# Sums of weight quarters in a decoder layer's token mixing, made on VectorE instead of by accumulating DMAs

## The chip, the cores and the metric

The kernel runs on one core of a Trainium2 chip. The metric is the device time of one execution in microseconds. Three runs of the kernel before gave 1376.22, 1376.38 and 1378.35 us; the median is 1376.38 us. One further execution was recorded by the hardware profiler: 1376.86 us, of which the span from the first to the last instruction is 1375.1 us. Everything below that has a place in time ("at 611.13 us") is counted from the start of that span.

## The reference

One decoder layer: a half-step feed-forward, token mixing in three gated branches, a second half-step feed-forward, with a normalisation before and behind each. There are 512 tokens, a model width of 1024 and a feed-forward width of 2816, all in float32.

```python
def swiglu(x, w_gu, w_down):
    g, u = jnp.split(x @ w_gu, 2, axis=-1)
    return (jax.nn.silu(g) * u) @ w_down

def token_mixing(u, mem, w_in, ...):
    proj = u @ w_in
    hq, hf, hi, hog, dcols, mq, gl = jnp.split(proj, SPLITS, axis=-1)
    o_hg = rmsnorm(hgrn2(hq, hf, hi, lb), hg_norm_w)
    ...
    y_dil = dilated_attention(dcols)
    y_mem = memory_attention(mq, mem, mem_norm_w, w_mem_kv)
    ...
    y = (gates[:, :, 0] * (y_hg @ w_br_hg)
         + gates[:, :, 1] * (y_dil @ w_br_dil)
         + gates[:, :, 2] * (y_mem @ w_br_mem))
    return y @ w_out

def reference(...):
    h = h + 0.5 * rmsnorm(swiglu(rmsnorm(h, ffn1_pre_w), ffn1_w_gu, ffn1_w_down), ffn1_post_w)
    u = rmsnorm(h, mix_pre_w)
    y = token_mixing(u, mem, w_in, ...)
    h = h + rmsnorm(y, mix_post_w)
    h = h + 0.5 * rmsnorm(swiglu(rmsnorm(h, ffn2_pre_w), ffn2_w_gu, ffn2_w_down), ffn2_post_w)
```

What matters here are the wide projections `x @ w_gu` and `u @ w_in`.

## The kernel before

**Seven products for a pair of columns.** Most of both projections is done for two blocks of 128 weight columns at a time (`pair`). The 1024 x 256 piece of the weights is seen as 2 x 2 quarters of 512 x 128: `a11` and `a12` are the two halves of the first column block, `a21` and `a22` those of the second. The tokens are split in two halves of 256 as well, and seven products of quarters take the place of eight. Four of the seven need a sum of quarters as their weight: `s1 = a21 + a22`, `s3 = a21 + a11`, `s2 = s1 + a11`, `s4 = s2 + a12`. Products 1, 2 and 4 take `a11`, `a12` and `a22` as they are; 5, 6, 3 and 7 take s1, s2, s4 and s3. Product j is asked for in the order 1, 6, 5, 7, 2, 3, 4.

**Splitting.** For precision each weight quarter is split into a high part (ScalarE, line 161) and the rest (VectorE, line 162 by way of `tt`, line 158), and each product is 12 matmuls of 256 columns (lines 353 to 355): high by high, high by low, low by high, for four pieces of 128 rows. A pair is thus 84 such matmuls, 7 splits, and some additions of its results (`pair` and `pair_out`, lines 358 to 392), from which other work goes on.

**Loading.** `wops` (line 285) loads a pair: `st` (a11 and a12, 512 KB, 4 buffers, shared with other weights) and `sh` (a22, 256 KB, 2 buffers) come through SyncE's DMA queue. The quarter a21 is loaded twice, into two buffers of the five named `sum`, and GpSimd then issues an accumulating DMA onto each (line 302), which adds a22 to the one and a11 to the other; these are s1 and s3. s2 and s4 are made by VectorE when they are asked for (line 309). `pairs` (line 321) calls `wops` one pair ahead of the pair that is being computed.

**What calls it.** `ffn` uses pairs for the feed-forward weights (20 pairs in each of two), `hgrn_pair`, `dil_pair`, the step of the memory queries and `branch` for the columns of `w_in` (32 pairs in all). In `dil_pair` (line 912) six pairs follow each other; each makes the queries and keys of one attention head, and the scores (line 340, four small matmuls a head, tile `px`) follow a few microseconds behind each pair. Behind the last pair of a group the author calls for the outstanding scores at once, before anything else:

```python
            for i, (hd, nb, s0, s12, st0, st1) in enumerate(heads):
                self.need(*scores[i])
                t_dil.append(self.spawn(self.dil_values(hd, s0, s12, st0, st1, v, y_dil)))
```

`branch` has a pair and then 24 matmuls of 512 columns for two outputs.

**What sets the order.** The author writes the order of tasks; side tasks (scores, softmax, HGRN2 steps) are generators that are woken after so many microseconds of matmuls have been issued (`tick`, the table LAT). From that program a scheduler lays out one list of instructions per engine. On the chip each engine and each DMA queue works strictly through its own list: an instruction that waits holds up all that stand behind it on the same engine. GpSimd's list holds the accumulating DMAs, the small DMAs that exchange softmax statistics between heads' layouts (tiles `x` and `ot`, lines 756 to 761), the powers of the normalisation (line 181) and some memsets.

**Names in the trace.** `sum<-sh` is the accumulating DMA that makes s1, `sum<-st` on POOL the one that makes s3, `sum<-sum,st` on DVE an addition for s2 or s4. `w<-st,w`, `w<-sum,w` and `w<-sh,w` are the low parts of splits; `w<-sh,w`, the split of a22, is the last use of an `sh` buffer and frees it. `s<-s,s`, `s<-s,ps` and `s<-ps,s` of 256 columns are additions of a pair's results. `ps<-xhi,w` and the like are the matmuls of a pair, `px<-s,s` (line 340) among others those of the scores.

## Time and profile before

| | |
|---|---|
| median of 3 runs (lowest to highest) | 1376.38 us (1376.22 to 1378.35) |
| profiled execution | 1376.86 us |
| its span | 1375.1 us |
| TensorE (PE) busy | 1333.8 us, 97% |
| VectorE (DVE) busy | 1015.6 us, 74% |
| ScalarE (ACT) busy | 742.5 us, 54% |
| GpSimd (POOL) busy | 161.9 us, 12% |
| bytes moved by DMA | 210.95 MB |

The token mixing runs from about 350 to 990 us, with its first normalisation at 355 to 390 us, the two groups of `dil_pair` at about 575 to 653 us and 700 to 774 us on TensorE, the pairs of the memory queries between them, and the three calls of `branch` from 774 us. The rest is feed-forward. Busy time of TensorE overlaps from one matmul to the next, so an engine that is 97% busy can still lose a little time in gaps that the waits don't list; SyncE only issues DMAs, and has no busy time.

### The profile page before, as it was taken

How to read it: one execution, taken by the hardware profiler on the slowest of the kernel's cores; microseconds unless marked ns; L12 is line 12 of the kernel's file. 1: busy time of each engine (PE TensorE's matmuls, PEld its weight loads, DVE VectorE, ACT ScalarE, POOL GpSimd, SP SyncE). 2: the span in 40 equal slices, each digit the busy share in tenths (PEclk: the TensorE clock that was granted, in tenths of full speed). 3: DMA queues.
4: the chain of work that ended last, by engine and by line, in shares of the span. 5: the costliest groups of instructions: out<-in, count | busy, mean ns of one | idle time of the engine just before them, and what ended most of it. 6: DMA issues, size and time to landing. Idle time of an engine off the chain costs nothing.

```text
span 1375.1 us, 24568 instructions
## 1 busy us (share of the span) xinstructions
PE 1333.8 (97%) x9197; PEld 1236.2 (90%) x9197; DVE 1015.6 (74%) x1932; ACT 742.5 (54%) x1527; POOL 161.9 (12%) x204
## 2 busy tenths in 40 slices
PE   6999999999999999998999999999999999999997
PEld 6999999999788888897899999999889999999995
DVE  6877777777787875576877787787478877777765
ACT  6665544555466755354645665565366655445541
POOL 1111111110111110111201211010021111111101
PEclk9999999999999999999999999999999999999999
DMA  9676565555547535576546666665465875656513
GB/s 268 146 174 184 150 153 140 147 149 160 188 116 214 154 92 171 156 156 158 119 124 164 147 146 162 147 161 139 129 208 122 189 187 148 153 138 153 140 47 138
DMA packets 264238, 210.95 MB, mean 153 GB/s; under 512 B 10645, under 2 KB 216886, under 8 KB 264118
## 3 DMA queue, kind: packets, MB, share of 16 engines
q1 hardware_dynamic: 241142, 168.41, 41.2%
q0 software_dynamic: 21248, 37.82, 16.8%
q10 hardware_dynamic: 1728, 3.15, 0.6%
q8 instruction: 72, 1.18, 0.4%
q14 instruction: 48, 0.39, 0.1%
HBM read 162.12 MB, written 9.47 MB: 125 GB/s over the span
## 4 chain that ended last, share of the span: by engine, by line
PE 43%; DVE 4%; DMA 3%; issue 2%; ACT 1%; POOL 1%; SPq 0%; DVEq 0%; POOLq 0%; ACTq 0%
PE ps L353 8%; PE ps L355 8%; PE ps L354 8%; PE ps L334 3%; PE ps L333 3%; PE ps L335 3%; PE px L334 2%; PE px L333 2%; PE px L335 2%; PE px L340 2%; DVE s L158 1%; DVE w L158 1%; DMA sh<-in_w_in_dram 1%; PE px L344 1%; DMA sum<-sh 1%
## 5 line engine op out<-in xcount | busy, mean ns | idle before, releaser
L161 ACT ACTIVATE w<-sum 128x512 fp32r<-128x512 f32 x288 | 180.2, 631 | 221.0 <-PE ps L354 171.8
L158 DVE TENSOR_TENSOR w<-sum,w 128x512 fp32r<-128x512 f32 x288 | 196.2, 687 | 83.4 <-ACT w L161 81.7
L353 PE MATMUL ps<-xhi,w 128*128 128x256 f32 x864 | 247.1, 286 | 1.9 <-ACT s L371 1.9
L355 PE MATMUL ps<-xhi,w 128*128 128x256 f32 x864 | 245.7, 284 | 0.0
L354 PE MATMUL ps<-xlo,w 128*128 128x256 f32 x864 | 245.2, 284 | 0.0
L161 ACT ACTIVATE w<-st 128x512 fp32r<-128x512 f32 x260 | 163.3, 630 | 135.2 <-PE ps L354 97.1
L158 DVE TENSOR_TENSOR w<-st,w 128x512 fp32r<-128x512 f32 x260 | 177.0, 687 | 42.0 <-ACT w L161 40.5
L158 DVE TENSOR_TENSOR s<-s,s 128x256 f32<-128x256 f32 (+3 forms) x316 | 176.7, 564 | 17.2 <-ACT s L161 4.2
L353 PEld LDWEIGHTS ps<-xhi,w 128*128 128x128 f32 x864 | 166.2, 192 | 4.8 <-ACT s L371 2.1
L354 PEld LDWEIGHTS ps<-xlo,w 128*128 128x128 f32 x864 | 166.3, 192 | 2.4 <-issue 0.2
L355 PEld LDWEIGHTS ps<-xhi,w 128*128 128x128 f32 x864 | 166.4, 193 | 0.0
L302 POOL DMA_DIRECT2D sum<-st x72 | 62.8, 872 | 618.7 <-DVE s L158 312.4
L158 DVE TENSOR_TENSOR sum<-sum,st 128x512 f32<-128x512 f32 x144 | 99.1, 688 | 42.5 <-issue 31.8
L158 DVE TENSOR_TENSOR s<-s,ps 128x256 f32<-128x256 f32 (+1 forms) x194 | 92.1, 476 | 33.8 <-PE ps L335 25.9
L333 PE MATMUL px<-s,s 128*128 128x512 f32 x288 | 112.6, 391 | 0.0
L334 PE MATMUL px<-s,s 128*128 128x512 f32 x288 | 112.5, 391 | 0.0
L335 PE MATMUL px<-s,s 128*128 128x512 f32 x288 | 112.1, 389 | 0.0
L302 POOL DMA_DIRECT2D sum<-sh x72 | 63.2, 877 | 272.3 <-DMA sh<-in_w_in_dram 104.3
L353 PE MATMUL ps<-t3hi,w 128*128 128x256 f32 x288 | 82.6, 287 | 0.7 <-DVE s L158 0.7
L353 PE MATMUL ps<-t4hi,w 128*128 128x256 f32 x288 | 82.2, 285 | 0.0
L354 PE MATMUL ps<-t3lo,w 128*128 128x256 f32 x288 | 82.1, 285 | 0.0
L353 PE MATMUL ps<-t2hi,w 128*128 128x256 f32 x288 | 81.9, 284 | 0.0
(185 smaller groups left out, 3417.7 us busy)
## 6 DMA issues: line engine op xcount, KB each, us to landing
st<-in_ffn_w_gu_dram SPq DMA_DIRECT2D x48, 512.0 KB, 4.7
st<-in_w_in_dram SPq DMA_DIRECT2D x48, 512.0 KB, 3.9
st<-in_ffn_w_down_dram SPq DMA_DIRECT2D x44, 512.0 KB, 4.0
sum<-in_ffn_w_gu_dram SPq DMA_DIRECT2D x80, 256.0 KB, 3.4
sum<-sh POOLq DMA_DIRECT2D x72, 256.0 KB, 3.8
sum<-st POOLq DMA_DIRECT2D x72, 256.0 KB, 3.8
sum<-in_w_in_dram SPq DMA_DIRECT2D x64, 256.0 KB, 3.1
sh<-in_ffn_w_gu_dram SPq DMA_DIRECT2D x40, 256.0 KB, 3.6
```

What stands on the lines that cost most here:

```text
L158: self.pin(self.nc.vector.tensor_tensor(out=out, in0=a, in1=b, op=op))
L161: self.pin(self.nc.scalar.activation(hi, src, AF.Copy))
L302: self.nc.gpsimd.dma_start(out=u, in_=x, accum_op=ALU.add)
L333: mm(out, lhsT=lhs[0], rhs=rhs[0], start=first, stop=False)
L334: mm(out, lhsT=lhs[0], rhs=rhs[1], start=False, stop=False)
L335: mm(out, lhsT=lhs[1], rhs=rhs[0], start=False, stop=last)
L340: self.nc.tensor.matmul(out, lhsT=lhsT, rhs=rhs, start=start, stop=stop, **k)
L344: self.nc.tensor.transpose(out, in_, self.ident)
L353: mm(out, lhsT=lh, rhs=rh, start=first and k == 0, stop=False, skip_group_check=True)
L354: mm(out, lhsT=lh, rhs=rl, start=False, stop=False, skip_group_check=True)
L355: mm(out, lhsT=ll, rhs=rh, start=False, stop=k == 3, skip_group_check=True)
```

## The change

In the token mixing `wops` loads a21 once, into one `sum` buffer, and issues no accumulating DMA. When s1 is asked for, VectorE makes it as `a21 + a22` in a buffer of its own, and when s3 is asked for, VectorE adds a11 to a21 in place. The feed-forward calls `pairs` with `by_load=True` and keeps its two loads and two accumulating DMAs. For 32 pairs this takes away 32 loads of 256 KB, 64 accumulating DMAs of 256 KB and their 64 entries in GpSimd's list, and adds 64 VectorE additions of 128 x 512.

```diff
--- before.py
+++ after.py
@@ -282,7 +282,7 @@
                 out += [(hi[:, i, :], lo[:, i, :]) for i in range(per)]
         return out
 
-    def wops(self, w, c1, c2):
+    def wops(self, w, c1, c2, by_load):
 
 
 
@@ -296,15 +296,23 @@
         def new_sum():
             return self.wpool.tile([P, 4, P], F32, tag="sum", bufs=NSUM, name=f"sum{self.uid()}")
 
-        for n, x in (("s1", a22), ("s3", a11)):
-            u = new_sum()
-            self.bring(u, quarter(0))
-            self.nc.gpsimd.dma_start(out=u, in_=x, accum_op=ALU.add)
-            sums[n] = u
+        if by_load:
+            for n, x in (("s1", a22), ("s3", a11)):
+                u = new_sum()
+                self.bring(u, quarter(0))
+                self.nc.gpsimd.dma_start(out=u, in_=x, accum_op=ALU.add)
+                sums[n] = u
+        else:
+            a21 = sums["a21"] = new_sum()
+            self.bring(a21, quarter(0))
 
         def total(n):
+            if n == "s3" and n not in sums:
+                total("s1")
+                self.tt(a21, a21, a11, ALU.add)
+                sums[n] = a21
             if n not in sums:
-                a, b = {"s2": ("s1", a11), "s4": ("s2", a12)}[n]
+                a, b = {"s1": ("a21", a22), "s2": ("s1", a11), "s4": ("s2", a12)}[n]
                 u = new_sum()
                 self.tt(u, total(a), b, ALU.add)
                 sums[n] = u
@@ -318,11 +326,11 @@
             return ops[j]
         return get
 
-    def pairs(self, specs):
+    def pairs(self, specs, by_load=False):
 
         ahead = None
         for x in specs:
-            now, ahead = ahead, self.wops(*x)
+            now, ahead = ahead, self.wops(*x, by_load)
             if now:
                 yield now
         yield ahead
@@ -417,7 +425,7 @@
         y = [[self.slot() for _ in range(2)] for _ in range(NT)]
         gw = self.col_tiles(w_gu, 0, plain)
         uw = self.col_tiles(w_gu, DFF, plain)
-        pairs = self.pairs([(w_gu, f * P, DFF + f * P) for f in range(plain, NF)])
+        pairs = self.pairs([(w_gu, f * P, DFF + f * P) for f in range(plain, NF)], True)
 
         def swiglu(sg, su, act):
             nc.scalar.activation(sg, sg, AF.Silu)
```

The scheduler lays the lists out anew. Three places of it follow; the numbers behind the names tell buffers and tiles apart.

VectorE's list at the end of the first `dil_pair` group, from the split of a22 of its last pair (tile sh1549 before, sh1548 after), which frees an `sh` buffer, to the sums of the pair that is loaded into that buffer next (sh1646 in both, a pair of memory queries). Before:

```order
L158 TENSOR_TENSOR w1599_7713<-sh1549_7446,w1598_7712 128x512
L158 TENSOR_TENSOR s1546_7442<-s1554_7456,ps1562_7496 128x4x64
L158 TENSOR_TENSOR w1615_7801<-st1607_7787,w1614_7800 128x512
L158 TENSOR_TENSOR s1547_7443<-ps1565_7514,s1554_7456 128x4x64
L158 TENSOR_TENSOR w1620_7823<-sum1618_7819,w1619_7822 128x512
L158 TENSOR_TENSOR w1623_7841<-sum1609_7791,w1622_7840 128x512
L158 TENSOR_TENSOR s1579_7596<-s1578_7595,ps1582_7614 128x256
L158 TENSOR_TENSOR w1626_7859<-sum1610_7794,w1625_7858 128x512
L158 TENSOR_TENSOR sum1660_8010<-sum1647_7944,st1645_7940 128x512
```

After:

```order
L158 TENSOR_TENSOR w1599_7701<-sh1548_7432,w1598_7700 128x512
L158 TENSOR_TENSOR s1545_7428<-s1552_7438,ps1561_7480 128x4x64
L158 TENSOR_TENSOR w1614_7785<-st1607_7775,w1613_7784 128x512
L158 TENSOR_TENSOR s1546_7429<-ps1564_7498,s1552_7438 128x4x64
L158 TENSOR_TENSOR w1620_7809<-sum1617_7803,w1619_7808 128x512
L158 TENSOR_TENSOR sum1660_7994<-sum1647_7931,sh1646_7929 128x512
L158 TENSOR_TENSOR sum1647_7931<-sum1647_7931,st1645_7927 128x512
L158 TENSOR_TENSOR w1623_7827<-sum1618_7804,w1622_7826 128x512
L158 TENSOR_TENSOR s1578_7581<-s1577_7580,ps1581_7599 128x256
L158 TENSOR_TENSOR w1626_7846<-sum1609_7779,w1625_7845 128x512
L158 TENSOR_TENSOR sum1659_7993<-sum1660_7994,st1645_7927 128x512
L158 TENSOR_TENSOR sum1658_7992<-sum1659_7993,st1645_7927 128x512
```

Between the freeing split and the first sum of the later pair stood seven instructions, and now stand four; before, that first sum read `sum1647`, a finished s1; now it reads the loaded quarter and `sh1646` itself. Two splits and a result addition that stood ahead of the sums now stand behind s1 and s3.

GpSimd's list in the same group, the fifth pair's sums (sum1519, sum1520) among its rows. Before:

```order
L302 DMA sum1520_7297<-st1517_7290 128x512
L756 DMA x0_0_7750<-st0_0_6804 128x4x2
L761 DMA ot1_0_7755<-x0_0_7750 128x8
L302 DMA sum1519_7294<-sh1518_7292 128x512
L302 DMA sum1551_7451<-st1548_7444 128x512
L302 DMA sum1550_7448<-sh1549_7446 128x512
L302 DMA sum1609_7791<-sh1608_7789 128x512
L302 DMA sum1610_7794<-st1607_7787 128x512
L302 DMA sum1647_7944<-sh1646_7942 128x512
```

After:

```order
L711 TENSOR_TENSOR hr_1404_6778<-hss_1403_6777,mhalf_86 128x4
L764 DMA x0_0_7738<-st0_0_6798 128x4x2
L769 DMA ot1_0_7743<-x0_0_7738 128x8
L765 DMA x1_0_7739<-st1_0_6799 128x8
L764 DMA x0_1_7767<-st0_1_6806 128x4x2
L768 DMA ot0_0_7742<-x1_0_7739 128x4x2
L769 DMA ot1_1_7772<-x0_1_7767 128x8
```

The DMAs of the statistics (x0, x1, ot0, ot1) stood between accumulating DMAs, and `ot1_0`, which waits for `x0_0` to land, stood ahead of `sum1519`, the s1 of a pair. Now they follow each other, with nothing of the weights in between.

VectorE's list in the normalisation at the start of the token mixing, tiles 1 and 2 of four. Before:

```order
L180 TENSOR_SCALAR v_883_4370<-ss0_879_4364,ss1_881_4367 128x1
L158 TENSOR_TENSOR sum1002_4862<-sum989_4824,st987_4820 128x512
L190 SCALAR_TENSOR_TENSOR s885_4374<-s859_4296,r_884_4371,s877_4358 128x512
L190 SCALAR_TENSOR_TENSOR s886_4376<-s860_4297,r_884_4371,s878_4359 128x512
L158 TENSOR_TENSOR s5_120<-s5_120,ps903_4436 128x512
L158 TENSOR_TENSOR s3_118<-s3_118,s867_4312 128x512
L180 TENSOR_SCALAR v_893_4413<-ss0_888_4392,ss1_891_4409 128x1
L158 TENSOR_TENSOR s4_119<-s4_119,s868_4313 128x512
L244 SCALAR_TENSOR_TENSOR s861_4298<-s3_118,r_894_4414,s861_4298 128x512
```

After:

```order
L180 TENSOR_SCALAR v_883_4370<-ss0_879_4364,ss1_881_4367 128x1
L158 TENSOR_TENSOR sum1000_4854<-sum1001_4855,st987_4820 128x512
L190 SCALAR_TENSOR_TENSOR s885_4374<-s859_4296,r_884_4371,s877_4358 128x512
L190 SCALAR_TENSOR_TENSOR s886_4376<-s860_4297,r_884_4371,s878_4359 128x512
L158 TENSOR_TENSOR sum999_4853<-sum1000_4854,st987_4820 128x512
L158 TENSOR_TENSOR s3_118<-s3_118,s867_4312 128x512
L180 TENSOR_SCALAR v_893_4413<-ss0_888_4392,ss1_891_4409 128x1
L158 TENSOR_TENSOR s4_119<-s4_119,s868_4313 128x512
L244 SCALAR_TENSOR_TENSOR s861_4298<-s3_118,r_894_4414,s861_4298 128x512
```

An addition for s2 stood in this chain; now s2 and s4 of the first pair stand in it, and its s3 stands further on, beside tile 4. The addition of `ps903` moved a few rows back.

## Rows read from the trace of the kernel before

**Rows 1.** The profile page: span, the row of busy times, and a row of the DMA queues (queue, kind: packets, MB, share of 16 engines; q0 carries GpSimd's DMAs).

```profile
span 1375.1 us, 24568 instructions
...
PE 1333.8 (97%) x9197; PEld 1236.2 (90%) x9197; DVE 1015.6 (74%) x1932; ACT 742.5 (54%) x1527; POOL 161.9 (12%) x204
...
q0 software_dynamic: 21248, 37.82, 16.8%
```

**Rows 2.** Busy time by stretch: the first normalisation of the token mixing with the pairs behind it, the `dil_pair` groups with the memory queries between them, the three branches. Columns: stretch, its us, then busy us and number of instructions of PE, PEld, DVE, ACT and POOL, the granted clock, the share of DMA time, GB/s.

```profile
355.00:465.00 110.00, 105.19 (x653) 92.34 (x653) 93.44 (x171) 74.04 (x159) 16.49 (x22) 1.00 0.57 154
595.00:775.00 180.00, 170.08 (x1309) 162.07 (x1308) 134.78 (x322) 94.77 (x239) 28.69 (x36) 0.98 0.62 148
780.00:985.00 205.00, 205.00 (x1402) 190.98 (x1401) 153.94 (x303) 112.64 (x211) 19.05 (x23) 1.00 0.56 141
```

**Rows 3.** What TensorE waited for from 595 to 775 us: its instruction, what ended the wait, us in total, times, longest.

```profile
PE px L340 <- DVE s L158: 8.0, 5, 4.7
PE px L340 <- ACT s L577: 1.1, 1, 1.1
PE ps L353 <- DVE s L158: 0.7, 1, 0.7
```

**Rows 4.** The same from 355 to 465 us (from 780 to 985 us the view has no row).

```profile
PE px L344 <- DVE s L190: 4.7, 5, 1.4
```

**Rows 5.** What VectorE waited for from 595 to 775 us (same columns; "issue" is a wait that the profile shows no releaser for).

```profile
DVE sum L158 <- issue: 21.1, 7, 4.1
```

**Rows 6.** The instructions on the `sum` tiles from 595 to 775 us, with their counts and durations in ns (least, median, most), and the time from issue to landing of their DMAs.

```profile
L158 DVE TENSOR_TENSOR sum<-sum,st x25: 680/692/694, 595.4 to 771.1; 128x512 f32<-128x512 f32 x25
...
L302 POOL DMA_DIRECT2D sum<-sh x12: 845/850/923, 605.6 to 764.9; - x12
...
DMA to landing us min/median/max: 2.7/3.9/7.9
```

**Rows 7.** SyncE's DMA issues (start, us, what) from 594 us.

```profile
597.01 0.37 SPq L151 DMA_DIRECT2D sh<-in_w_in_dram  x1
```

**Rows 8.** GpSimd's instructions in order of time: start, us, what [idle time before it <- what ended it].

```profile
605.01 0.57 POOL L761 DMA_DIRECT2D ot<-x  x1 [7.03 <-DMA x<-st]
605.57 0.92 POOL L302 DMA_DIRECT2D sum<-sh  x1
...
640.87 0.85 POOL L302 DMA_DIRECT2D sum<-sh  x1 [8.94 <-DVE s L158]
```

**Rows 9.** VectorE's, from 596 us.

```profile
596.29 0.68 DVE L158 TENSOR_TENSOR w<-sh,w 128x512 fp32r<-128x512 f32 x1
...
611.13 0.69 DVE L158 TENSOR_TENSOR sum<-sum,st 128x512 f32<-128x512 f32 x1 [4.11 <-issue]
```

**Rows 10.** VectorE's, from 636 us.

```profile
636.65 0.68 DVE L158 TENSOR_TENSOR w<-sh,w 128x512 fp32r<-128x512 f32 x1
...
637.77 0.68 DVE L158 TENSOR_TENSOR w<-st,w 128x512 fp32r<-128x512 f32 x1
638.37 0.59 DVE L158 TENSOR_TENSOR s<-ps,s 128x256 f32<-128x256 f32 x1
638.88 1.28 DVE L158 TENSOR_TENSOR w<-sum,w 128x512 fp32r<-128x512 f32 x2
...
640.42 0.68 DVE L158 TENSOR_TENSOR w<-sum,w 128x512 fp32r<-128x512 f32 x1
644.18 1.42 DVE L158 TENSOR_TENSOR sum<-sum,st 128x512 f32<-128x512 f32 x2 [3.08 <-issue]
...
650.10 0.59 DVE L158 TENSOR_TENSOR s<-ps,s 128x256 f32<-128x256 f32 x1
```

**Rows 11.** TensorE's, at 645 to 651 us.

```profile
645.04 0.28 PE L353 MATMUL ps<-t4hi,w 128*128 128x256 f32 x1
...
645.40 0.28 PE L353 MATMUL ps<-xhi,w 128*128 128x256 f32 x1
...
650.83 1.41 PE L340 MATMUL px<-s,s 128*128 128x128 f32 x5 [4.67 <-DVE s L158]
```

**Rows 12.** GpSimd's powers of the normalisation.

```profile
363.15 0.86 POOL L181 TENSOR_TENSOR r<-v,mhalf 128x1 f32<-128x1 f32 x1 [2.92 <-DVE v L180]
366.92 0.55 POOL L181 TENSOR_TENSOR r<-v,mhalf 128x1 f32<-128x1 f32 x1 [2.91 <-DVE v L180]
```

**Rows 13.** VectorE's beside them.

```profile
362.92 0.68 DVE L158 TENSOR_TENSOR s<-s,s 128x512 f32<-128x512 f32 x1
...
366.69 0.68 DVE L158 TENSOR_TENSOR s<-s,ps 128x512 f32<-128x512 f32 x1
```

**Rows 14.** DMA issues of the whole run: out<-in, queue, operation, times, KB each, median us from issue to landing.

```profile
sum<-in_w_in_dram SPq DMA_DIRECT2D x64, 256.0 KB, 3.1
...
sh<-in_w_in_dram SPq DMA_DIRECT2D x32, 256.0 KB, 3.4
```

**Rows 15.** SyncE's, from 749 us.

```profile
749.38 0.37 SPq L151 DMA_DIRECT2D sh<-in_w_in_dram  x1
```

**Rows 16.** GpSimd's, from 753 us.

```profile
753.34 0.85 POOL L302 DMA_DIRECT2D sum<-sh  x1 [11.29 <-DVE w L158]
```

**Rows 17.** VectorE's, from 759 us.

```profile
759.63 0.69 DVE L158 TENSOR_TENSOR sum<-sum,st 128x512 f32<-128x512 f32 x1 [3.48 <-issue]
```

## The prediction

> **What bounds the kernel now.** I read the page first, then busy time by stretch, then the waits of the stretches in which TensorE stands idle, then the order of time around the longest of them. TensorE is busy for 1333.8 of 1375.1 us [rows 1]; a faster kernel can only come from its gaps. By stretch [rows 2] there is none from 780 to 985 us (205.00 of 205.00), 4.8 us from 355 to 465 (105.19 of 110.00) and 9.9 us from 595 to 775 (170.08 of 180.00). The reader should see that the new additions run in all three, but that only the last two have time to win or lose on TensorE at once.

> From 595 to 775 us nearly all of the gap is TensorE waiting for a result that VectorE makes: 8.0 us in front of score matmuls and 0.7 us in front of a pair's matmul [rows 3]. VectorE is not out of time there (134.78 of 180 us busy [rows 2]); it stands still itself, for 21.1 us in 7 waits, in front of additions for s2 or s4 [rows 5]. In order of time one sees what it stands for. At 611.13 us it had waited 4.11 us [rows 9]. The `sh` load of that pair was issued at 597.01 [rows 7], but GpSimd issued the accumulating DMA onto it only at 605.57, because `ot<-x` in front of it in GpSimd's list had waited 7.03 us for a statistics DMA [rows 8]. At 644.18 VectorE had waited 3.08 us [rows 10]: split of a22 at 636.65, load, accumulating DMA at 640.87 (GpSimd had waited for its releaser [rows 8]), and its landing. At 759.63 it had waited 3.48 us [rows 17] for a load issued at 749.38 [rows 15] and an accumulating DMA issued at 753.34 [rows 16]. Behind each of these stand a pair's result additions, and behind those the scores. The largest bill is at 650.83: TensorE waits 4.67 us [rows 11], since VectorE, busy without a stop from 644.18, gets to the last result addition only at 650.10 [rows 10].

> **What goes.** For each pair of the mixing, the step between the landing of a22 and s1: GpSimd's 0.85 us and some 3.9 us to landing [rows 6], 4.75 us, plus whatever stood ahead in GpSimd's list. In its place comes one addition on VectorE, 0.69 us [rows 6]; behind other work an addition takes 0.60 us from start to start (637.77 to 638.37 [rows 10]). At 611.13 the gain is larger: the load of 597.01 with a median of 3.4 us [rows 14] is there at 600.4, so s1 and s2 would be made near 602, some 9 us earlier. From then on VectorE has a lead again. The splits run far ahead of TensorE: the a22 split of 636.65 belongs to the product whose matmuls end at 645.4 [rows 10, 11], so a lead of this size reaches the results.

> What is left of TensorE's 8.7 us? The scores behind the last pair of each group are called for at once, so TensorE then always waits for that pair's last two result additions, two of 0.59 us spaced 0.52 us [rows 10] behind a matmul that ends some 0.2 us after 645.4, about 1 us each time. At the two group ends (one is the 4.67 us) I leave 0.9 us each, 1.8 us. The rest, 6.9 us, goes. As bounds: at most all 8.7 us and the 1.1 us behind ScalarE's exponentials, 9.8 us [rows 3]; at least what a count of the instructions at 644.18 gives, if no lead is built. There a22 lands at 640.87 (GpSimd starts at that moment); s1, s3, two splits, s2, s4, two more splits are eight at 0.60 us, and the other instructions up to the last addition took 650.69 - 644.18 = 6.5 us less four at 0.60 (two sums, two splits), 4.1 us. That ends at 640.87 + 4.8 + 4.1 = 649.8, plus 0.34 us for the result addition that moved behind s1, 650.1, against 650.69: 0.6 us. For two group ends that is 1.2 us. I take 6.9, near the upper end, because the row of 605.57 shows a delay that isn't in that count and goes in full.

> **What comes.** 64 additions at 0.60 us, 38 us of VectorE's time. From 780 to 985 us, 24 of them for 12 pairs, 14.4 us, beside 51 us in which VectorE is idle and TensorE waits for nothing [rows 2, 4]: nothing, and if that cover were gone, up to 14 us. From 595 to 775 us another 24 for the 12 pairs that the accumulating DMAs count [rows 6], 14.4 us, against 21.1 us of waiting that they replace: that is inside the 6.9 us. In the normalisation at 355 to 390 us one more sum (s4) stands in the chain of tiles 1 and 2 and one (s3) beside tile 4. VectorE has hardly a pause there (93.44 of 110 us [rows 2]) and TensorE already waits for its scaled rows, 4.7 us [rows 4]. Two sums at 0.60 us are 1.2 us late in full; bounds 0 (both fall into pauses for GpSimd's power) and 2.4 us (four sums, if s1's of the first two pairs hit it as well). I take 1.2. The load and the buffers cost nothing: one `sum` buffer per pair is filled ahead instead of two, and 32 loads go from SyncE's queue, whose next entries then start sooner.

> [...] GpSimd's power took 0.86 us at 363.15 with an addition of two SBUF tiles beside it, and 0.55 us at 366.92 beside one with a PSUM input [rows 12, 13]. [...]

> **Sum.** -6.9 + 1.2 = -5.7 us on the profiled execution's own 1376.86 us, 1371.2. The median of the runs is 0.48 us lower; 1376.38 - 5.7 = 1370.7 us.

> **Rivals.**
> *The sums wait elsewhere.* s1 now stands four instructions behind the split that frees the buffer of its own a22, where s2 stood seven behind. The load takes 640.87 - 636.65 = 4.2 us from that split, four instructions about 2 us; so VectorE may stand still 2.2 us at s1 instead of 3.08 us at s2, with two more sums to make. For it: the lead stays nil if each pair is held by this ring of split, load, s1. Then the lower bound holds, -1.2 + 1.2 = 0: 1376.4 us. Against it: TensorE's pace, 0.12 us per matmul (three from 645.04 to 645.40 [rows 11]), 84 in a pair, 10.1 us, with scores about 11, while the ring by my count of VectorE's list has 11 us too.

> *VectorE becomes the bound* (the slower side). Place: the 12 pairs from 595 to 775 us. In the same ring a pair loses 2.2 us to its load plus 1.2 us to the two sums, 3.4, against the 21.1/12 = 1.8 us that it loses now: 1.6 us more a pair, 19 us. TensorE now pays 8.7 of VectorE's 21.1 us, 41%; of 19 us that is 8 us, and with the normalisation's 1.2: 1385.6 us. It decides once VectorE's loss per pair exceeds 1.8 us, that is when a load is issued less than about 1.8 us of VectorE's own work too late. Against it: 45 us of idle VectorE in that stretch [rows 2].

> *All of it goes.* The full 9.8 us and no price in the normalisation: 1366.6 us. For it: the powers leave pauses there. Against it: the scores that are called for at once.

> That the change does not do what it says is out: the lists show s1 and s3 on VectorE and no accumulating DMA between the statistics DMAs.

> **How the numbers follow.** The forecast has 0.55, with a range of its own of 1368.8 to 1373.5; all of it 0.11; the sums wait elsewhere 0.20; VectorE the bound 0.14. 0.2% of 1376 us is 2.75 us, about what a measurement of this kernel can tell from no change. Faster than 1373.6: 0.55 + 0.11 = 0.66. Within: 0.20. Slower: 0.14. The range from 1366.0 to 1378.0 takes in all cases but the slower one and the edges of the forecast.

> **What would show it.** VectorE's waits in front of sums (21.1 us) should fall under 10 in the same stretch, TensorE's waits for VectorE from 8.7 to about 2, with no wait over 1.2 us in front of scores; GpSimd's list should show no `sum` before the second feed-forward's; the normalisation's 4.7 us should be about 6. A wait of VectorE in front of a sum that reads `sh` of over 2 us in most pairs would prove me wrong, and so would new waits of TensorE from 780 to 985 us.

## The result and the profile after

The changed kernel takes 1367.38 us (median of 4 runs, 1364.92 to 1368.56) against 1376.3 us for the kernel before (4 runs, 1374.45 to 1378.35): 8.9 us less by the medians. The ratio on record is 0.9921, 95% interval 0.9898 to 0.9945, or 7.6 to 14.0 us less, with 10.9 us in the middle; the quotient of the two medians is 0.9935, inside the interval. Forecast were 5.7 us less (1370.7 us, own range 1368.8 to 1373.5, whole range 1366.0 to 1378.0); 0.9921 of the 1376.38 us from which it was reckoned are 1365.5 us. The sign and the place were right; the size was too small. The profiled execution took 1367.62 us, 9.24 us less than that of before.

The page of the kernel after (span, busy times, the row of GpSimd's DMA queue), answering [rows 1]:

```profile
span 1365.8 us, 24324 instructions
...
PE 1331.6 (97%) x9197; PEld 1233.0 (90%) x9197; DVE 1050.7 (77%) x1996; ACT 742.2 (54%) x1527; POOL 107.0 (8%) x140
...
q0 software_dynamic: 12032, 21.04, 9.4%
```

VectorE has 64 instructions and 35 us more, GpSimd 64 fewer. TensorE has the same 9197 matmuls. The same three stretches by busy time, with the columns of [rows 2]:

```profile
355.00:465.00 110.00, 105.21 (x660) 92.66 (x659) 99.06 (x182) 75.37 (x162) 7.95 (x12) 1.00 0.38 117
595.00:775.00 180.00, 175.34 (x1368) 166.93 (x1367) 156.42 (x377) 101.09 (x258) 10.61 (x16) 1.00 0.36 97
780.00:985.00 205.00, 205.00 (x1385) 190.20 (x1384) 158.86 (x286) 110.24 (x207) 1.79 (x2) 1.00 0.37 108
```

TensorE's gap from 595 to 775 us has shrunk from 9.9 to 4.7 us, and two columns further on the granted clock reads 1.00 where it read 0.98. What TensorE and VectorE still wait for there, answering [rows 3, 5]:

```profile
PE px L348 <- DVE s L158: 2.2, 3, 1.0
PE px L348 <- ACT s L585: 1.6, 1, 1.6
PE ps L341 <- ACT w L161: 0.7, 1, 0.7
```

```profile
DVE sum L158 <- DMA sh<-in_w_in_dram: 4.0, 4, 1.7
```

Waits for VectorE fell from 8.7 to 2.2 us, and VectorE's own waits in front of sums from 21.1 to 4.0 us. The longest wait, 4.67 us at 650.83 [rows 11], is 0.95 us now, as the forecast for a group's end had it. TensorE's rows at that place in the kernel after, and the memory attention behind it:

```profile
642.95 1.13 PE L348 MATMUL px<-s,s 128*128 128x128 f32 x8 [0.95 <-DVE s L158]
...
656.23 2.20 PE L348 MATMUL px<-s,s 128*128 128x256 f32 x8 [1.02 <-DVE s L158]
...
660.42 1.13 PE L348 MATMUL px<-s,s 128*128 128x256 f32 x4 [1.64 <-ACT s L585]
```

The last two rows are where some of the gain is given back: TensorE arrives earlier at the memory attention and waits there for exponentials and for VectorE.

What 0.98 meant is seen when the stretch behind 650.83 is cut finely. The kernel before:

```profile
645.00:650.00 5.00, 1.16 (x10) 0.95 (x8) 5.00 (x12) 1.50 (x7) 0.00 (x0) 0.90 0.49 129
650.00:655.00 5.00, 4.17 (x19) 4.20 (x20) 2.77 (x7) 3.54 (x14) 1.36 (x2) 0.50 0.55 162
655.00:660.00 5.00, 5.00 (x41) 5.00 (x40) 1.95 (x9) 3.90 (x13) 1.90 (x4) 0.92 0.23 55
```

and its matmuls in order of time:

```profile
653.11 0.41 PE L354 MATMUL ps<-xlo,w 128*128 128x256 f32 x1
653.32 0.41 PE L355 MATMUL ps<-xhi,w 128*128 128x256 f32 x1
...
655.97 0.28 PE L353 MATMUL ps<-t2hi,w 128*128 128x256 f32 x1
656.09 0.28 PE L354 MATMUL ps<-t2lo,w 128*128 128x256 f32 x1
```

A clock of 0.50 is half of full speed. TensorE had done almost nothing for 4.67 us; then it works for five microseconds with 0.21 us from matmul to matmul, where 0.12 us is its pace before and after.

The trace lists the same 9197 matmuls in both kernels. With each numbered in order of time, the start of the one before less the start of the one after says how far ahead the kernel after is at each point. It compares by number, so where the order of work differs a small change need not be lost time. This ledger, in us, read where it changes by more than 0.1:

| stretch (time before) | lead at its end | change |
|---|---|---|
| to 355, first feed-forward | 1.1 | +1.1 |
| 355 to 387, normalisation | -0.3 | -1.4 |
| 387 to 465 | 1.3 | +1.6 |
| 595 to 650.8, waits of the first group | 7.9 | +6.6 |
| 650.8 to 656, half-speed clock | 10.1 | +2.3 |
| 656 to 669, memory attention | 8.1 | -2.1 |
| 669 to 772, end of the second group | 9.6 | +1.5 |
| 772 to 985 | 8.6 | -1.0 |
| to the last matmul | 8.0 | -0.6 |
| to the end of the span | 9.3 | +1.3 |

### The profile page after: what moved, and what is told of

Same layout as the page of the kernel before. It is cut to its first block, busy times and chain, and to the rows that moved or that the text cites. A ratio compares the mean times of both kernels' runs of the same rounds, so it can differ in the third digit from the quotient of the medians.

```text
span 1365.8 us, 24324 instructions
## 1 busy us (share of the span) xinstructions
PE 1331.6 (97%) x9197; PEld 1233.0 (90%) x9197; DVE 1050.7 (77%) x1996; ACT 742.2 (54%) x1527; POOL 107.0 (8%) x140
## 4 chain that ended last, share of the span: by engine, by line
PE 87%; DVE 6%; issue 3%; DMA 2%; ACT 1%; POOL 1%; SPq 0%; POOLq 0%; DVEq 0%; ACTq 0%
PE ps L361 17%; PE ps L363 17%; PE ps L362 17%; PE ps L341 6%; PE ps L342 6%; PE ps L343 6%; PE px L341 5%; PE px L342 5%; PE px L343 5%; PE px L348 4%; DVE s L158 2%; PE px L352 1%; DVE w L158 1%; POOL r L181 1%; DVE s L244 1%
## 5 line engine op out<-in xcount | busy, mean ns | idle before, releaser
L158 DVE TENSOR_TENSOR sum<-sum,st 128x512 f32<-128x512 f32 x176 | 120.4, 687 | 10.9 <-issue 5.0
L361 PE MATMUL ps<-t1hi,w 128*128 128x256 f32 x288 | 81.7, 284 | 0.0
L363 PE MATMUL ps<-t1hi,w 128*128 128x256 f32 x288 | 81.6, 283 | 0.0
L362 PE MATMUL ps<-t2lo,w 128*128 128x256 f32 x288 | 81.5, 283 | 0.0
```

Source lines behind the costliest of these rows:

```text
L158: self.pin(self.nc.vector.tensor_tensor(out=out, in0=a, in1=b, op=op))
L361: mm(out, lhsT=lh, rhs=rh, start=first and k == 0, stop=False, skip_group_check=True)
L362: mm(out, lhsT=lh, rhs=rl, start=False, stop=False, skip_group_check=True)
L363: mm(out, lhsT=ll, rhs=rh, start=False, stop=k == 3, skip_group_check=True)
```

## The experiments

Each group of four had its own runs of the kernel before beside it, with medians of 1378.84, 1378.86 and 1380.68 us. Ratios and their 95% intervals are to these, as on record; each lies within 0.0014 of the quotient of the medians.

**1. Where the gain is: the change in the groups alone, and everywhere else alone.**

On the kernel after, `by_load=True` is added to the calls that keep their DMAs: first in `hgrn_pair` and `branch`,

```diff
-            f, q, o = [self.project2(x) for x in self.pairs([(w_in, c + 2 * hp * P, c + 2 * hp * P + P) for c in (C_HF, C_HQ, C_HOG)])]
+            f, q, o = [self.project2(x) for x in self.pairs([(w_in, c + 2 * hp * P, c + 2 * hp * P + P) for c in (C_HF, C_HQ, C_HOG)], True)]
...
-        pairs = self.pairs([(w_in, c + d * P, c + d * P + P) for d in range(0, KD, 2)])
+        pairs = self.pairs([(w_in, c + d * P, c + d * P + P) for d in range(0, KD, 2)], True)
```

then, in the other kernel, in `dil_pair` (not printed) and for the memory queries instead:

```diff
...
-                mq = self.pairs([(w_in, C_MQ + hp * 2 * P, C_MQ + hp * 2 * P + P)])
+                mq = self.pairs([(w_in, C_MQ + hp * 2 * P, C_MQ + hp * 2 * P + P)], True)
```

> The change in the two dil_pair groups and the memory queries alone (14 pairs); HGRN2's pairs and branch keep their accumulating DMAs. Theory A, read from a ledger of TensorE's instructions in both traces: the gain lies in TensorE's waits at the ends and between the pairs of the groups and in the half-speed clock behind the longest of them. Then this kernel is 7 to 9 us faster than the kernel before. Rival B, less DMA traffic and GpSimd work in the whole mixing: 14 of 32 pairs, 3 to 4 us faster. Rival C, the normalisation and HGRN2's pairs gain as well: 5 to 7 us.

1366.55 us, 0.9913 (0.9889 to 0.9936), or 8.8 to 15.3 us less: more than the 7 to 9 us of Theory A, whose upper end the interval just takes in.

> The reverse: VectorE's sums in HGRN2's pairs and in branch (18 pairs), accumulating DMAs in the dil_pair groups and the memory queries. Theory A: within 1 us of the kernel before, and the 4.7 us wait with its half-speed clock is still there. Rival B: 4 to 5 us faster. The prediction's price of the normalisation: 1.2 us slower.

1376.61 us, 0.9985 (0.9971 to 1.0000). Theory A holds: 14 of the 32 pairs carry the whole gain, 9 to 15 us by these runs; the other 18 at most 4 us and perhaps nothing. The long wait is still there in the second kernel, with the half-speed clock behind it, 0.21 us from matmul to matmul from 650.96 to 652.03 us:

```profile
648.90 2.05 PE L348 MATMUL px<-s,s 128*128 128x128 f32 x8 [4.79 <-DVE s L158]
```

```profile
650.00:655.00 5.00, 5.00 (x35) 5.00 (x35) 3.64 (x8) 3.29 (x11) 1.38 (x2) 0.78 0.39 113
```

**2. Is it the head of GpSimd's list?** The prediction took a value near its upper bound because of the 7.03 us for which `ot<-x` held up a sum at 605.57 [rows 8].

```diff
-            self.nc.gpsimd.dma_start(out=u, in_=x, accum_op=ALU.add)
+            self.acc = self.nc.gpsimd.dma_start(out=u, in_=x, accum_op=ALU.add).ins
...
-        nc.gpsimd.dma_start(out=ot0, in_=x1.rearrange("(j p) c -> p j c", p=P))
-        nc.gpsimd.dma_start(out=ot1, in_=x0.rearrange("(p a) c -> p a c", a=4))
+        with self.tc.issue_after(self.acc):
+            nc.gpsimd.dma_start(out=ot0, in_=x1.rearrange("(j p) c -> p j c", p=P))
+            nc.gpsimd.dma_start(out=ot1, in_=x0.rearrange("(p a) c -> p a c", a=4))
```

> The kernel before, with the statistics load ot<-x of a group's first head placed behind the next pair's accumulating DMAs in GpSimd's list, so that no sum stands behind its wait (605.57 us in the trace of before). If the head of GpSimd's list is what delays the group: the 4.1 us wait of VectorE at 611 us goes, the lead lasts to the end of the group, and the time falls by 4 to 7 us. If the step of the accumulating DMA and the ring of sh buffers holds each pair: the wait at 611 us goes but the later ones (644, 759 us) stay, and the time falls by 0 to 1.5 us.

1378.18 us, 0.9992 (0.9975 to 1.0008): nothing. GpSimd's rows of this kernel, VectorE's first addition behind them, and the scores at the group's end:

```profile
600.72 0.86 POOL L302 DMA_DIRECT2D sum<-sh  x1 [5.29 <-DMA sh<-in_w_in_dram]
...
607.92 0.89 POOL L762 DMA_DIRECT2D ot<-x  x1
```

```profile
608.30 0.69 DVE L158 TENSOR_TENSOR sum<-sum,st 128x512 f32<-128x512 f32 x1 [3.32 <-issue]
```

```profile
648.43 2.05 PE L340 MATMUL px<-s,s 128*128 128x128 f32 x8 [5.16 <-DVE s L158]
```

The sum is issued as soon as its `sh` is there, and now `ot<-x` stands behind it. VectorE still waits 3.32 us, and the group ends with a wait of 5.16 us. The DMA issues of this kernel from 596 to 612 us (times, KB, median us to landing) say why:

```profile
s<-v SPq DMA_DIRECT2D x2, 256.0 KB, 8.2
...
sum<-sh POOLq DMA_DIRECT2D x1, 256.0 KB, 7.5
```

The accumulating DMA took 7.5 us to land, beside two loads of values of 8.2 us each. In the kernel before, it was the load that was late (its issues from 596 to 612 us):

```profile
sh<-in_w_in_dram SPq DMA_DIRECT2D x1, 256.0 KB, 7.5
sum<-sh POOLq DMA_DIRECT2D x1, 256.0 KB, 5.5
```

Issued at 597.01 [rows 7], it landed at 604.5, so `ot<-x` kept the sum of 605.57 back by 1.1 us at most, not by the 5 us that follow from the prediction's median of 3.4 us. So a place in GpSimd's list was not what VectorE waited for; the prediction read the instruction that stood there as the cause of the delay. Both expectations had the wait at 611 us go, and it stayed.

**3. Which sum, and is it the ring of buffers?** Two kernels split the change by sums; a third leaves both sums with the DMA and gives `sh` a third buffer. The first, on the kernel after:

```diff
-            a21 = sums["a21"] = new_sum()
+            u = sums["s1"] = new_sum()
+            self.bring(u, quarter(0))
+            self.nc.gpsimd.dma_start(out=u, in_=a22, accum_op=ALU.add)
+            a21 = new_sum()
             self.bring(a21, quarter(0))
```

> The kernel after, but s1 of the mixing by a loaded quarter and an accumulating DMA as in the kernel before; s3 on VectorE. Theory A: what holds each pair is the step from the landing of a22 to s1 (accumulating DMA, 0.85 us and 3.9 us to landing), so nearly all of the gain is lost: 0 to 3 us faster than the kernel before, and VectorE's waits in front of s2 from 595 to 775 us stay over 12 us. Rival B: the DMA traffic counts (half of it is gone): 4 to 5 us faster. Rival C: the scores and the order of VectorE's list count, not the sums: 7 to 9 us faster.

1380.82 us, 1.0006 (0.9991 to 1.0021). VectorE's waits in front of sums from 595 to 775 us:

```profile
DVE sum L158 <- issue: 9.9, 3, 3.9
DVE sum L158 <- DMA sum<-in_w_in_dram: 8.6, 5, 3.5
DVE sum L158 <- DMA sum<-sh: 5.7, 3, 2.4
```

They add up to 24.2 us, and the scores at the group's end wait 5.4 us:

```profile
PE px L351 <- DVE s L158: 6.4, 3, 5.4
```

Nothing is gained. The kernel doesn't price the step to s1 alone: 8.6 of the 24.2 us are waits for the loaded a21, in front of s3, which VectorE makes here; the other 15.6 us are still above the 12 us of Theory A. The second, on the kernel after:

```diff
             self.bring(a21, quarter(0))
+            u = sums["s3"] = new_sum()
+            self.bring(u, quarter(0))
+            self.nc.gpsimd.dma_start(out=u, in_=a11, accum_op=ALU.add)
```

> The reverse: s1 on VectorE, s3 of the mixing by an accumulating DMA. Theory A: the gain is there in full, 7 to 10 us faster than the kernel before, with no half-speed clock at 649 us. Rival B (traffic): 4 to 5 us faster. Rival C: as the kernel after, 7 to 10 us, for both kernels of this pair.

1364.13 us, 0.9879 (0.9857 to 0.9902): at least the whole gain; the interval of the kernel after, 0.9898 to 0.9945, overlaps it a little. The same views, VectorE's sums first, then TensorE's waits:

```profile
DVE sum L158 <- DMA sh<-in_w_in_dram: 0.5, 1, 0.5
```

```profile
PE px L351 <- ACT s L588: 1.7, 1, 1.7
PE px L351 <- DVE s L158: 0.6, 2, 0.4
```

No clock is at half speed at 649 us, as expected (0.12 us from matmul to matmul), but behind the wait for ScalarE it is, with 0.21 us from 657.86 to 659.35 us:

```profile
655.90 1.95 PE L351 MATMUL px<-s,s 128*128 128x256 f32 x4 [1.72 <-ACT s L588]
```

```profile
655.00:660.00 5.00, 4.10 (x17) 3.75 (x18) 4.16 (x17) 2.97 (x13) 0.83 (x1) 0.66 0.77 162
```

The third, on the kernel before:

```diff
-NSLOT = 37
+NSLOT = 36
...
-        a22 = self.stage.tile([P, 4, P], F32, tag="st2", bufs=2, name=f"sh{self.uid()}")
+        a22 = self.stage.tile([P, 4, P], F32, tag="st2", bufs=3, name=f"sh{self.uid()}")
```

> The kernel before with three sh buffers instead of two (and 36 slots instead of 37, to make room). If the ring of two sh buffers (split of a22, load, accumulating DMA, s2) sets the pace, the load starts a pair earlier, VectorE's waits in front of sums fall from 21 us to under 8 and the time falls by 5 to 9 us without a sum moved. If the accumulating DMA's own 4 to 8 us in loaded queues are the cause, the waits stay over 12 us: 0 to 3 us faster. A slot fewer could cost up to 2 us.

1372.25 us, 0.994 (0.992 to 0.996). Again VectorE's sums, then TensorE:

```profile
DVE sum L158 <- DMA sum<-sh: 6.3, 2, 4.1
```

```profile
PE px L340 <- ACT s L577: 3.7, 1, 3.7
PE px L340 <- DVE s L158: 3.6, 2, 3.4
```

Theory A holds. The step from the landing of a22 to s1 holds each pair in a ring of split, load, s1 and s2. Take the step away and the waits go; give the ring a third buffer and two thirds of them go (21.1 to 6.3 us), without a sum moved. Traffic is no explanation of the gain: the first kernel had one of a pair's two accumulating DMAs less, and it brought nothing; the third had all of them, and it was 5.5 to 11.0 us faster than the kernel before. s3 is not in the ring; left to the DMA, it spares VectorE an addition, and VectorE waits 0.5 us instead of 4.0.

**4. The clock.** A first trial put matmuls that compute nothing into the 4.67 us wait of the kernel before.

```diff
...
             sp = self.paux((P, 4, P))
+            for _ in range(fill):
+                nc.tensor.matmul(sp[:, 0:2, :], lhsT=self.xhi[0][:, 0, :P], rhs=self.xhi[0][:, 0, :HT], start=True, stop=True)
             for a in range(4):
...
+                    scores[i].append(self.spawn(self.dil_scores(nb, g, q, k, s0 if g == 0 else s12, st0, 36 if (hp, g, i) == (0, 2, 1) else 0)))
```

> The kernel before, with 36 matmuls of 256 columns (some 0.12 us each, 4.3 us) put in front of the last scores of the first group, into the PSUM tile that these overwrite: work for TensorE in the 4.67 us wait, which changes nothing that is computed. If the half-speed clock from 649 to 656 us is the result of the wait and costs some 2.3 us: the granted clock stays at full speed there and the time falls by 2 to 2.5 us. If the clock has another cause or costs nothing: no change, or up to 1 us slower where the fillers end behind the wait.

1389.38 us, 1.0074 (1.0049 to 1.0099): a miss, since the scheduler laid the lists out around 4.5 us of new work and moved the long wait to the next pair.

```profile
643.68 4.48 PE L731 MATMUL px<-xhi 128*128 128x256 f32 x36
649.25 1.13 PE L340 MATMUL px<-s,s 128*128 128x128 f32 x8 [1.10 <-DVE s L158]
...
660.69 0.58 PE L353 MATMUL ps<-xhi,w 128*128 128x256 f32 x1 [4.57 <-ACT s L364]
```

```profile
645.00:650.00 5.00, 3.90 (x34) 3.73 (x33) 4.11 (x10) 3.10 (x13) 0.57 (x1) 1.00 0.49 137
650.00:655.00 5.00, 5.00 (x44) 5.00 (x43) 1.89 (x3) 2.40 (x7) 1.55 (x2) 1.00 0.51 135
...
660.00:665.00 5.00, 2.93 (x12) 2.64 (x12) 4.93 (x21) 2.87 (x12) 0.52 (x1) 0.66 0.79 156
```

The clock goes with the wait, though: full from 645 to 655 us, where it was 0.90 and 0.50, and down right behind the new wait of 4.57 us. The price can't be read from this kernel. The second trial goes the other way and puts a wait into the kernel after, beside a further run of the kernel after itself.

```diff
-                self.mm(sp[:, a, :], q[:, a, :], k[:, a, :])
+                self.last_score = nc.tensor.matmul(sp[:, a, :], lhsT=q[:, a, :], rhs=k[:, a, :], start=True, stop=True).ins
...
                         self.pair_out(r, views(q), views(k))
+                        if (hp, g, i) == (0, 2, 1):
+                            o, perm2 = views(k)[1]
+                            for _ in range(8):
+                                self.tt(o, perm2(r[4]), perm2(r[1]), ALU.subtract)
...
+                    with self.tc.issue_after(self.last_score):
+                        qs = self.project2(next(mq))
```

> The kernel after once more, beside the three others and on their chip, as their measure. As before: 8 to 10 us faster than the kernel before, no half-speed clock from 600 to 1350 us.

1369.87 us, 0.9919 (0.9897 to 0.9941), or 8.1 to 14.2 us less.

> The kernel after with the last result addition in front of the last scores of the first group made nine times instead of once (the same numbers each time) and the next pair's matmuls kept behind these scores: eight additions of some 0.5 us more, so TensorE's wait of 1.1 us there becomes about 5 us, as long as the 4.67 us wait of the kernel before. Theory A: the half-speed clock of the kernel before from 649 to 656 us belongs to that wait. Then it comes back behind the wait, the matmuls there start 0.2 us apart or more instead of 0.12, and the kernel is 4 us (the wait) plus 1.5 to 3 us slower than the kernel after. Rival: the clock there had another cause: no half speed, 4 us slower.

1373.46 us, 0.9952 (0.9937 to 0.9966). TensorE's row at the place, and the clock by stretch:

```profile
646.60 2.05 PE L739 MATMUL px<-s,s 128*128 128x128 f32 x8 [6.40 <-DVE s L158]
```

```profile
640.00:645.00 5.00, 0.20 (x2) 0.00 (x0) 4.90 (x10) 4.95 (x18) 1.30 (x2) 0.71 0.59 175
645.00:650.00 5.00, 3.40 (x16) 3.43 (x17) 3.90 (x9) 0.00 (x0) 1.31 (x2) 0.50 0.25 44
650.00:655.00 5.00, 5.00 (x35) 5.00 (x35) 3.72 (x14) 2.72 (x8) 0.00 (x0) 0.76 0.24 68
```

The wait came out longer than the 5 us meant, and the half-speed clock is back. So it belongs to the wait, and the rival falls. Against the profile of the kernel after, the ledger shows 6.1 us lost at the wait, and 2.0 us more until the clock is full again; 3.1 us of it come back in the memory attention, where no wait of TensorE is listed now. That is in part why the medians are only 3.6 us apart: waits of one place are paid in part by waits of the next.

**5. VectorE's room, and a better version.** VectorE's sums in the feed-forward as well; then s1 on VectorE and s3 by DMA in every pair; then that with every second head of the memory attention held back.

```diff
-        pairs = self.pairs([(w_gu, f * P, DFF + f * P) for f in range(plain, NF)], True)
+        pairs = self.pairs([(w_gu, f * P, DFF + f * P) for f in range(plain, NF)])
...
-        yield LAT['mem0']
+        yield LAT['mem0'] + 3.0 * (hd % 2)
```

> VectorE's sums in the feed-forward too: 40 more pairs, 80 more additions of 0.6 us, 48 us of VectorE's time in stretches in which it is busy some 73% and TensorE hardly waits. If VectorE has the room: within 2 us of the kernel after (1367 us). If the feed-forward's VectorE is what TensorE waits for next: 3 to 15 us slower than the kernel after.

1365.86 us, 0.9897 (0.9877 to 0.9917). The other 80 additions (VectorE is busy for 1095.1 instead of 1050.7 us, 80% of the span) cost nothing that these runs can tell.

> s1 on VectorE in the mixing and in the feed-forward, s3 by an accumulating DMA in both. If only the step between a22 and s1 matters: at least as fast as the same in the mixing alone (0.988 of the kernel before), 13 to 16 us faster than the kernel before and 3 to 6 us faster than the kernel after. If the feed-forward misses the finished s1: 2 to 5 us slower than that.

1363.17 us, 0.9871 (0.9847 to 0.9895), 6.7 us less than the kernel after beside it, and no run of the one lies among those of the other.

> The same with the scores of every second head of the memory attention held back by 3 us of matmuls, so that they don't stand in TensorE's list ahead of the exponentials whose PSUM tile they need (a wait of 1.6 us in the kernel after). If that wait and what stands behind it are lost time: 1 to 2 us faster than the kernel without it. If the heads then meet the next pair: no change or 1 us slower.

1362.2 us, 0.9863 (0.9839 to 0.9887). TensorE's waits from 340 to 775 us in it:

```profile
PE px L355 <- DVE s L190: 3.5, 4, 1.4
PE px L351 <- ACT s L588: 0.8, 1, 0.8
PE px L351 <- DVE s L158: 0.6, 2, 0.4
```

Both beat both kernels. Between the two, the 1 us of the last edit is not more than their measurement can tell.

## Why the prediction was right or wrong

*The step that failed is the sum's missing term.* The sum had waits (-6.9) and the normalisation (+1.2), and no row for TensorE's clock: the half speed behind the 4.67 us wait was put at nothing, and no reason was given. The profile of before had the sign in [rows 2], 0.98 from 595 to 775 us, and the text passed over it: 0.02 of 180 us is 3.6 us of full-speed time. The ledger has 2.3 us of it, from 650.8 to 656 us, and the delay experiment shows that a wait brings it (6.40 us, then 0.50 from 645 to 650 us). With it, the terms of the sum are -8.0 us; the medians say -8.9, the ratio -10.9, and the profiles -9.3 by their spans. The rest of these 9.3 us is made of smaller misses that partly cancel: the normalisation's stretch gave 0.2 where 1.2 us were to be lost (1.4 more), the groups without the clock gave 6.0 for 6.9, 1.6 us went behind 772 us, and 2.4 us came in two places that the change doesn't touch (below).

*595 to 775 us, -6.9.* The waits of TensorE for VectorE went from 8.7 to 2.2 us, 6.5 us: right in size. The two group ends keep 0.95 and 0.2 us, for which 0.9 each were left. Not foreseen was that a faster TensorE arrives earlier at what it needs next: by the waits 1.2 us more for ScalarE (1.1 to 2.3 us), by the ledger 2.1 us in the memory attention, the 1.02 us for VectorE at 656.23 among them.

*Its reasons.* The ring of split, load, accumulating DMA and s1 was right, and the experiments on s1, s3 and the third buffer show it. The head of GpSimd's list, for which the value was put near the upper bound, was wrong: without it nothing changed. That s1 of this pair would come much earlier was right all the same: by the accumulating DMA it landed at 611.05 us (605.57 + 5.5), and in the kernel after VectorE makes it here:

```profile
599.43 0.69 DVE L158 TENSOR_TENSOR sum<-sum,sh 128x512 f32<-128x512 f32 x1
```

There the `sh` load, issued at 595.58, had landed within 3.9 us instead of 7.5; why was not tested. The value came out because VectorE's s1 shortens every turn of the ring, which is luck as far as the reason given goes. The step itself was put too high, at 4.75 us: the 3.9 us count from the issue, as 605.57 + 5.5 shows, so GpSimd's 0.85 us are in them. The sum doesn't use this figure. Two more readings were off by a little: the last matmul before the 4.67 us wait ended at 646.16 us (650.83 less 4.67), not some 0.2 us behind 645.4, and a22 had landed some 0.6 us before 640.87, where GpSimd waited for VectorE, so the lower bound could have been that much higher at each group end.

*The normalisation, +1.2.* By the ledger it cost 1.4 us from 355 to 387 us, and TensorE's waits from 355 to 390 us rose from 2.0 to 3.7 us. Before, then after:

```profile
PE px L344 <- DVE s L190: 2.0, 3, 1.1
```

```profile
PE px L352 <- DVE s L190: 1.9, 2, 1.1
PE ps L342 <- DVE w L158: 1.8, 1, 1.8
```

But 1.6 us came back from 445 to 459 us, so the term was +1.2 and the measured change -0.2. The kernel with VectorE's sums here and not in the groups was 0 to 4.0 us faster than the kernel before, not 1.2 slower. [Rows 4] pools two places: 2.0 of its 4.7 us lie in the normalisation, the other 2.7 us in the same helper's transposes for the memory, and those fell to 1.0 us. The text took all five waits for the normalisation's. GpSimd's powers took 0.86 to 0.93 us in both traces where a VectorE instruction with two SBUF inputs was running as they started, and 0.55 to 0.57 us elsewhere. The change brought no more of the slower ones here: of the seven from 355 to 387 us six took 0.86 us before and five after.

*780 to 985 us, nothing.* Right: TensorE is busy for 205.00 of 205.00 us, and the lead, 9.2 us at 780, stays at 8.6 from 785 us on.

*Rivals.* "The sums wait elsewhere" named the wait that s1 now has, up to 2.2 us a pair; it is at most 1.7 us and 4.0 us in all. "VectorE becomes the bound" did not come, even with 44 us more. "All of it goes" gave 1366.6 us, nearest to the measured time, but for another reason: not all waits went, and the clock paid for the rest.

*What stays open.* Of the profiled difference, 1.1 us lie in the first feed-forward, where the profile of before has half a clock at 17 and at 65 us, with 0.21 us from matmul to matmul (of the 13 other profiles one has the first and none the second), and 1.3 us between the last matmul and the end, mostly the landing of the last store. The change doesn't touch either. How much of the 8.9 us such things are in a median was not settled: the mean clock of a run, side by side in the third group, was 0.990 to 0.997 for the kernel before (16 runs) and 0.995 to 0.997 for the kernel after (6 runs).

## What to carry to other kernels

TensorE's wait of 4.67 us had a second price here, 2.3 us for the work done at half speed behind it (0.50 from 650 to 655 us): cut a stretch whose granted clock reads below 1.00 into pieces, and put that loss into the sum beside the wait. A step that closes a ring of buffers is paid again at every turn of it (without it VectorE's waits fell from 21.1 to 4.0 us here); look for the one sum in the ring, and leave the others where they cost nothing. And when an instruction stands idle at the head of a queue, ask what the work behind it would still wait for.

## What the runs showed of the hardware

An accumulating DMA of 256 KB took 3.9 us from issue to landing in the median of the kernel before (595 to 775 us),

```profile
sum<-sh POOLq DMA_DIRECT2D x12, 256.0 KB, 3.9
```

and 7.5 us beside two loads of values in the kernel of the second experiment; the addition on VectorE that replaced it took 0.69 us.
